# Conditioning scale and shift of the first norm: two-column TensorE products in place of VectorE dot products

## The chip, the cores and the metric

The kernel runs on one core of one Trainium2 chip. The metric is the device time of one execution in microseconds (us). Profile times are us from the start of the span. Engines are named as the profile names them: PE is TensorE, DVE VectorE, ACT ScalarE, POOL GpSimd, SP SyncE, whose queue issues most loads.

## What is computed

Two token streams go through one layer, 1024 prompt tokens and 32 sample tokens, each stream with a conditioning vector `c` of 1024 values. The change touches only the first lines of the layer:

```python
def rmsnorm(x, g):
    return x * lax.rsqrt(jnp.mean(x * x, axis=-1, keepdims=True) + EPS) * g

def layer(x, c, S0, conv_prev, p):
    mod = (c @ w_mod + b_mod)[:, None, :]              # c: 1024, w_mod: 1024 x 6144
    sh1, sc1, g1, sh2, sc2, g2 = jnp.split(mod, N_MOD, axis=-1)
    h = rmsnorm(x, norm1_g) * (1 + sc1) + sh1
    m, S_new, buf = token_mixer(h, ...)                # first: h @ w_in
    ...
```

`sh1` and `sc1` are 1024 values for each stream. Everything that follows (a gated linear attention, a short convolution, a gated merge, a SwiGLU mixer) needs `h`.

## The kernel before, in words

Channels lie on the 128 partitions: the 1024 channels are 8 tiles (`KT`), and the 1056 tokens of both streams lie along the free dimension, in blocks of 384, 384 and 288. Every product with a large weight is made of three float32r products (`hi*hi`, `hi*lo`, `lo*hi`): ACT rounds a weight to its high half (`whi`, `hl`), POOL or DVE subtracts to get the low half (`wlo`, `hl`); activations are split likewise into two tiles (`xm`, `h`).

The 48 columns of `mod` (6 groups of 8 tiles of 128 channels) come from `mod_tile`. It loads 128 rows of the transposed `w_mod` (`wm`, 512 KB) and lets DVE take a dot product of 1024 elements along the free dimension with `cb`, the conditioning vector written out on all partitions. For the prompt's vector that copy is made by two PE products (`pscb`), for the sample's by a load.

The first stage goes through a list written by hand, `ORDER`. `x` loads a tile of tokens and squares it, `w` loads and splits a weight tile of the keys, `c` makes a scale column of the prompt (`scale_col`), `m` scales and splits an x tile (`scaled`, tiles `xm`), `g` is one step of the contraction for the keys, taken before the norm's factor is known (`kmajor`, seven PSUM banks `psk`, 21 products of 384 columns), `s0` sums the squares (`psq`), and `s1` spreads the reciprocal root over the partitions (`psb`, `rstd`). Then the `psk` banks are multiplied by `rstd` into `st`.

A second list, `ORDER2`, makes the eight shift columns of the prompt (`s`, `shift_col`), two weight tiles of the queries (`w`), and `h` for tile 0 to 7 (`h`: POOL multiplies x by `rstd`, ACT adds the shift and rounds, DVE makes the low half). Behind it stand five PSUM banks of `kmajor` over `h` (15 products a step) and two further query tiles (`late`, tiles `ps`, 48 products a tile). The sample's scale and shift columns are made after that (`scale_col(k, 1)`, `shift_col(k, 1)`), followed by the gate projection (`psa`) and the value products (`psv`), among which the other 32 columns of `mod` are made for both streams (`some_mods`, 64 dot products).

A scheduler orders the instructions of each engine; only the loads are held in the order of the program (`pin`). PSUM is two pools of four banks, `psm` and `psx`. The `wm` buffers are five, and some small weights and the masks share them.

Of the kernel before, what the change touches and what calls it, by code (L numbers as in the profile page):

```python
# [7 lines left out]
F32 = mybir.dt.float32  # L8
# [3 lines left out]
ALU = mybir.AluOpType  # L12

P = 128
D = 1024
KT = D // P
# [28 lines left out]
DGL = 4  # L45
SSETS = 1
DTB = 1
ORDER2 = "p0 p1 p2 p3 p4 p5 p6 p7 s0 s1 w0 s2 s3 w1 s4 h0 h1 h2 s5 h3 s6 h4 s7 h5 h6 h7 c1".split()
W_LO = ('dve', 'pool')
W1_LO = ('pool', 'dve', 'pool', 'pool')  # L50
ORDER = "x0 w0 c0 m0 x1 c1 m1 x2 w1 x3 c2 m2 x4 w2 w3 g0 c4 c3 g1 x5 m3 m4 x6 x7 s0 s1 g2 g3 c5 m5 c7 c6 m6 g4 m7 g5 g6 g7".split()

Q0, K0, G0, CB0, CC0, CH0, GA0, GB0 = 0, 4, 8, 16, 24, 32, 40, 48

# [14 lines left out]
def hybrid_trunk(  # L69
    ctx: ExitStack,  # L70
    tc: tile.TileContext,
    xT,
    c_row,
    w_modT,
    b_mod,
    norm_g,
# [21 lines left out]
    nc = tc.nc  # L98
# [4 lines left out]
    psm = ctx.enter_context(tc.tile_pool(name="psm", bufs=4, space=bass.MemoryType.PSUM))  # L103
    psx = ctx.enter_context(tc.tile_pool(name="psx", bufs=4, space=bass.MemoryType.PSUM))
# [16 lines left out]
    ones = const.tile([P, P], F32, name="ones")  # L121
    masks = const.tile([P, 2 * len(LEVELS) + 1, P], U8, name="masks")
    epst = const.tile([P, 1], F32, name="epst")
    bmod = const.tile([P, 48], F32, name="bmod")
    ngs = const.tile([P, 3, KT], F32, name="ngs")
# [3 lines left out]
    mods = const.tile([P, 2, 48], F32, name="mods")  # L129
# [4 lines left out]
    def mm(ps, lhsT, rhs, start, stop):  # L134
        nc.tensor.matmul(ps, lhsT, rhs, start=start, stop=stop)  # L135
# [13 lines left out]
    def nm(s):  # L149
        uid[0] += 1  # L150
        return f"{s}_{uid[0]}"
# [3 lines left out]
    def load(dst, src):  # L155
        ins = nc.sync.dma_start(dst, src)
        if pin[0]:
            tc.keep_in_program_order(ins)
# [32 lines left out]
    with tc.tile_pool(name="p1", bufs=1) as p1:  # L191
        SL = "s"
        NSL = 9
        cb = p1.tile([P, 2, D], F32, name="cb")
        b1 = const.tile([P, KT], F32, name="b1")
        am1 = const.tile([P, 2, KT], F32, name="am1")
# [6 lines left out]
        nc.vector.tensor_scalar(b1, bmod[:, 8:16], 1.0, None, op0=ALU.add)  # L203

        def cond(s):
            if s:
                load(cb[:, s, :], c_row[:, s * D : (s + 1) * D].to_broadcast([P, D]))
                return
            crow = p1.tile([1, D], F32, tag="wm", name=nm("crow"), bufs=5)
            load(crow, c_row[:, s * D : (s + 1) * D])  # L210
            for i in range(2):
                ps = psm.tile([P, 512], F32, tag="m", name=nm("pscb"))
                mm(ps, ones[0:1, :], crow[:, i * 512 : (i + 1) * 512], True, True)
                nc.vector.tensor_copy(cb[:, s, i * 512 : (i + 1) * 512], ps)

        pin[0] = True
        cond(0)

        def mod_tile(j, s=None):
            wm = p1.tile([P, D], F32, tag="wm", name=nm("wm"), bufs=5)  # L220
            load(wm, w_modT[j])
            for st in (0, 1) if s is None else (s,):
                junk = p1.tile([P, D], F32, tag="junk", name=nm("junk"), bufs=1)
                nc.vector.tensor_tensor_reduce(  # L224
                    junk, wm, cb[:, st, :], 1.0, 0.0, ALU.mult, ALU.add, mods[:, st, j : j + 1]
                )

        def scale_col(k, s):
            mod_tile(8 + k, s)
            nc.vector.tensor_scalar(  # L230
                am1[:, s, k : k + 1], mods[:, s, 8 + k : 9 + k], b1[:, k : k + 1], ngs[:, 0, k : k + 1],
                op0=ALU.add, op1=ALU.mult,
            )

        def shift_col(k, s):
            mod_tile(k, s)
            nc.vector.tensor_tensor(mods[:, s, k : k + 1], mods[:, s, k : k + 1], bmod[:, k : k + 1], op=ALU.add)

        HW = BO[2]
        xs, sqs, xm, ws = [], [], [], []  # L240
# [31 lines left out]
        def banks(keys):  # L272
            return {(i, b): ((psm, psx)[b]).tile([P, 512], F32, tag="mx"[b], name=nm("psk")) for i, b in keys}
# [3 lines left out]
        rstds = []  # L277

        def sums():
            psq = psx.tile([P, 512], F32, tag="x", name="psq")  # L280
            for c in range(9):
                n = min(P, T - c * P)
                for i, sq in enumerate(sqs):
                    mm(psq[:n, c : c + 1], sq[:, c * P : c * P + n], ones[:, 0:1], i == 0, i == len(sqs) - 1)
            nc.scalar.activation(msc[:, 0:8], psq[:, 0:8], AF.Sqrt, bias=epst, scale=1.0 / D)
            nc.scalar.activation(msc[:DS, 8:9], psq[:DS, 8:9], AF.Sqrt, bias=epst[:DS], scale=1.0 / D)
            nc.vector.reciprocal(msc, msc)
# [10 lines left out]
                nc.scalar.copy(rstd[:, c0 * P : c0 * P + w], psb[:, :w])  # L298

        pss = banks(((0, 0), (0, 1), (1, 0), (1, 1), (2, 0), (2, 1), (3, 0)))  # L300
        for item in ORDER:
            kind, k = item[0], int(item[1])
            if kind == "x":
                load_x(k)
            elif kind == "c":
                scale_col(k, 0)
            elif kind == "m":
                scaled(k)
            elif kind == "w":
                hl = [p1.tile([P, KT, P], F32R, name=nm("hl")) for _ in range(2)] if k == 3 else None  # L310
                ws.append(load_w(w_in[K0 + k], hl=hl, lo_eng=W1_LO[k]))
            elif kind == "g":
                kmajor(pss, ws, xm[k], k)
            elif kind == "s":
                (sums, spread)[k]()
# [16 lines left out]
        for i in range(4):  # L332
            tag, bufs = ("sq", 4) if i < 3 else (SL, NSL)
            stk.append(p1.tile([P, T], F32, tag=tag, name=nm("st"), bufs=bufs))
        for (i, b), t in pss.items():
            nc.vector.tensor_tensor(stk[i][:, blk(b)], t[:, : wd(b)], rstd[:, blk(b)], op=ALU.mult)

        ws2 = [ws[3]]
        for item in ORDER2:
            kind, k = item[0], int(item[1])  # L340
            if kind == "s":
                shift_col(k, 0)
            elif kind == "w":
                ws2.append(load_w(w_in[Q0 + k], lo_eng=W_LO[k]))
            elif kind == "c":
                cond(1)
            elif kind == "p":
                nc.scalar.activation(xs[k][:, :S], xs[k][:, :S], AF.Copy, scale=am1[:, 0, k : k + 1])
            else:
                hi, lo = (r1.tile([P, T + 2], F32R, tag="r1", name=nm("h")) for _ in range(2))  # L350
                h.append((hi, lo))
                xp, shk = xs[k][:, :S], mods[:, 0, k : k + 1]
                nc.gpsimd.tensor_tensor(xp, xp, rstd[:, :S], op=ALU.mult)
                nc.scalar.activation(hi[:, :S], xp, AF.Identity, bias=shk)
                nc.vector.scalar_tensor_tensor(
                    lo[:, :S], xp, shk, f(hi[:, :S]), op0=ALU.add, op1=ALU.subtract
                )
# [46 lines left out]
            gemm(w, h, ev, blocks=(0, 1))  # L404

        for k in range(KT):
            scale_col(k, 1)
            shift_col(k, 1)
            modulate_sample(k)

        A = p1.tile([6 * RANK, T], F32R, tag="sq", name="A", bufs=4)
        for b in range(NB):
# [3 lines left out]
            ps = psm.tile([P, 512], F32, tag="m", name=nm("psa"))  # L416
# [70 lines left out]
        for hd in range(H):  # L487
# [10 lines left out]
            for tt in range(9):  # L498
                n = P if tt < 8 else DS
                sl = slice(tt * P, tt * P + n)  # L500
                ps = psm.tile([P, 512], F32, tag="m", name=nm("psv"))
# [557 lines left out]
    def cols(q):  # L1059
        return slice(2 * q * CW, 2 * (q + 1) * CW)  # L1060
# [105 lines left out]
    for j in range(KT):  # L1166
        w = load_w(w_conv_out[j])
        for c in range(NCH):
# [3 lines left out]
            ps = psc()  # L1172
# [645 lines left out]
```

## Time and profile before

| | |
|---|---|
| median of 3 runs | 1935.99 us (1935.78 to 1937.6) |
| profiled execution, its own time | 1936.16 us |
| span of that execution | 1934.4 us |
| mean granted clock of PE | 0.98 |
| PE busy | 1834.0 us, 95% of the span |
| DVE busy | 1383.1 us, 71% |
| ACT busy, POOL busy | 788.0 us, 41%; 797.6 us, 41% |

Time and span differ by 1.8 us, which lies outside the first and the last instruction. A busy share is an average over stages with different limits. The change acts in the first 280 us, so the views below are of that stretch; they are to be read for who waits for whom there and for the clock that PE had.

### The profile page before, as it was taken

To read this page: it belongs to the slowest core of one execution; us is meant where nothing else is said; L and a number is where in the kernel's file an instruction comes from. 1 tells how busy PE (TensorE), PEld (TensorE's weight loads), DVE (VectorE), ACT (ScalarE), POOL (GpSimd) and SP (SyncE) were. 2 spreads that over 40 slices of the span, in tenths; PEclk is the share of its full clock that TensorE was granted. 3 is DMA by queue.
4 is the path that set the end of the run, shared out by engine and by line. 5 is a ranking of instruction groups with operands and counts; after the bars stand their busy time and mean duration, and the time that the engine had idled before them with its cause. 6 is when DMAs were issued, how large, how long until landed. Compare 5 with 4: busy or idle time off the path is not lost. (4 is left out here: it accounts for less than half of the span.)

```text
span 1934.4 us, 35506 instructions
## 1 busy us (share of the span) xinstructions
PE 1834.0 (95%) x13517; PEld 1808.9 (94%) x13517; DVE 1383.1 (71%) x2543; ACT 788.0 (41%) x1641; POOL 797.6 (41%) x649
## 2 busy tenths in 40 slices
PE   6799899999999979999999999899999999999997
PEld 5689889899999979999999999899999999999997
DVE  7999967786875378543114478779988988678865
ACT  5434344444443145544212256444444444322243
POOL 6754447574762352212433243113223222255574
PEclk9799999999999989999999999999999999999998
DMA  7586643322322217424854455213443434586522
GB/s 275 182 292 229 212 165 123 93 83 77 100 77 77 76 61 233 152 106 167 318 184 146 134 161 161 80 56 128 154 153 128 153 143 143 203 313 235 212 95 90
DMA packets 166269, 298.45 MB, mean 154 GB/s; under 512 B 20593, under 2 KB 81905, under 8 KB 166098
## 3 DMA queue, kind: packets, MB, share of 16 engines
q1 hardware_dynamic: 117170, 211.90, 33.7%
q10 hardware_dynamic: 48928, 84.27, 11.7%
q8 instruction: 106, 1.74, 0.4%
q14 instruction: 65, 0.53, 0.1%
HBM read 211.78 MB, written 84.33 MB: 153 GB/s over the span
## 5 line engine op out<-in xcount | busy, mean ns | idle before, releaser
L135 PE MATMUL ps<-h,whi 128*128 128x384 f32 (+2 forms) x1440 | 350.3, 328 | 5.7 <-DVE vst L518 3.6
L143 POOL TENSOR_TENSOR wlo<-raw,whi 128x512 fp32r<-128x512 f32 (+2 forms) x160 | 220.7, 1398 | 312.7 <-ACT whi L139 214.1
L1327 PE MATMUL psX<-op,wg 128*128 128x264 f32 (+1 forms) x2112 | 273.1, 286 | 6.5 <-DVE bz L1358 4.2
L1327 PEld LDWEIGHTS psX<-op,wg 128*128 128x128 f32 x2112 | 264.1, 189 | 9.2 <-DVE bz L1358 6.1
L135 PEld LDWEIGHTS ps<-h,whi 128*128 128x128 f32 x1440 | 256.2, 193 | 6.7 <-issue 3.9
L940 POOL TENSOR_TENSOR wg<-raw,wg 128x512 fp32r<-128x512 f32 x66 | 96.3, 1459 | 366.9 <-ACT wg L939 301.6
L135 PE MATMUL ps<-h,wlo 128*128 128x384 f32 (+2 forms) x720 | 236.7, 329 | 0.0
L135 PE MATMUL ps<-u,whi 128*128 128x264 f32 (+2 forms) x1064 | 225.2, 305 | 2.3 <-ACT whi L139 1.7
L135 PEld LDWEIGHTS ps<-u,whi 128*128 128x128 f32 x1064 | 175.3, 188 | 3.3 <-ACT whi L139 2.0
L135 PE MATMUL ps<-u,wlo 128*128 128x264 f32 (+2 forms) x532 | 162.1, 305 | 0.0
L224 DVE CUSTOM_DVE_ANT_0 junk<-wm,cb 128x1024 f32<-128x1024 f32 x96 | 152.9, 1593 | 5.5 <-DMA wm<-in_w_modT 4.0
L1327 PE MATMUL psV<-op,wg 128*128 128x264 f32 (+1 forms) x1056 | 138.0, 286 | 1.0 <-ACT wg L939 1.0
L135 PEld LDWEIGHTS ps<-h,wlo 128*128 128x128 f32 x720 | 138.4, 192 | 0.4 <-issue 0.2
L1052 PE MATMUL psH<-u,wg 128*128 128x264 f32 x1056 | 133.9, 286 | 2.7 <-ACT wg L939 2.7
L139 ACT CAST whi<-raw 128x512 fp32r<-128x512 f32 (+2 forms) x164 | 87.5, 578 | 116.5 <-PE ps L135 56.1
L1327 PEld LDWEIGHTS psV<-op,wg 128*128 128x128 f32 x1056 | 133.3, 189 | 1.3 <-ACT wg L939 1.3
L1052 PEld LDWEIGHTS psH<-u,wg 128*128 128x128 f32 x1056 | 131.2, 190 | 3.3 <-ACT wg L939 3.3
L939 ACT CAST wg<-d 128x512 fp32r<-128x512 f32 x132 | 81.4, 621 | 109.7 <-PE psV L1327 36.8
L940 DVE TENSOR_TENSOR wg<-d,wg 128x512 fp32r<-128x512 f32 x121 | 93.8, 777 | 42.7 <-ACT wg L939 42.5
L1052 PE MATMUL psH<-h,wg 128*128 128x264 f32 x792 | 101.9, 287 | 6.2 <-ACT d L945 6.2
L1608 PE MATMUL psX<-u,wg 128*128 128x264 f32 x768 | 106.2, 284 | 0.0
L1052 PEld LDWEIGHTS psH<-h,wg 128*128 128x128 f32 x792 | 99.3, 191 | 6.5 <-ACT d L945 6.5
(321 smaller groups left out, 4008.4 us busy)
## 6 DMA issues: line engine op xcount, KB each, us to landing
wm<-in_w_modT SPq DMA_DIRECT2D x64, 512.0 KB, 4.6
raw<-in_w_in SPq DMA_DIRECT2D x124, 256.0 KB, 3.1
op_d<-st ACTq DMA_DIRECT2D x56, 528.0 KB, 5.7
u<-op_d SPq DMA_DIRECT2D x56, 528.0 KB, 6.2
raw<-in_w_ffn_in SPq DMA_DIRECT2D x88, 256.0 KB, 3.2
u<-og_d SPq DMA_DIRECT2D x16, 528.0 KB, 8.5
raw<-in_w_o SPq DMA_DIRECT2D x32, 256.0 KB, 3.2
raw<-in_w_ffn_out SPq DMA_DIRECT2D x32, 256.0 KB, 5.3
```

The costliest lines, as they stand in the source:

```text
L135: nc.tensor.matmul(ps, lhsT, rhs, start=start, stop=stop)
L139: nc.scalar.copy(hi, raw)
L143: nc.gpsimd.tensor_tensor(lo, raw, f(hi), op=ALU.subtract)
L224: nc.vector.tensor_tensor_reduce(junk, wm, cb[:, st, :], 1.0, 0.0, ALU.mult, ALU.add, mods[:, st, j : j + 1])
L939: nc.scalar.copy(hi, src)
L940: lo_eng.tensor_tensor(lo, src, f(hi), op=ALU.subtract)
L1052: nc.tensor.matmul(bank[i][q], wt[l][:, k, :], h_operand(i, k, q, r), start=i in (B11, B21, T3) and k == 0 and n == 0, stop=k == 3 and n == 2,
L1327: nc.tensor.matmul(ps, l[:, k, :], r[:, k, :], start=first and k == 0 and i == 0, stop=k == 3 and i == 2, skip_group_check=True,)
L1608: nc.tensor.matmul(ps, w[l][:, k, :], o[k][:, r, c], start=first and k == 0 and i == 0, stop=k == n - 1 and i == 2, skip_group_check=True,)
```

## The change

The 16 columns of shift and scale leave `mod_tile`. Their part of `w_mod` comes in a second layout, `w_modP`, contraction on the partitions, and `cc` holds both conditioning vectors as two columns for each contraction tile. For one column tile PE makes 8 products of a 128 x 128 weight with a 128 x 2 operand, in float32 without a split, into two columns of a PSUM bank (`psd` for the scale, `psd2` for the shift). One small DVE instruction then finishes both streams. The sample's columns therefore come with the prompt's, and the 16 separate loads for them are gone. `psd` takes the fourth bank of `psx`; the sums of squares move into it, and `s1` moves behind `m7`, since `psb` needs that bank. Both rows of `cb` are now loaded (`c0 c1`).

```diff
-ORDER2 = "p0 ... s7 h5 h6 h7 c1".split()
+ORDER2 = "p0 ... s7 h5 h6 h7 c0 c1".split()
-ORDER = "... x6 x7 s0 s1 g2 g3 c5 m5 c7 c6 m6 g4 m7 g5 g6 g7".split()
+ORDER = "... x6 x7 s0 g2 g3 c5 m5 c7 c6 m6 g4 m7 s1 g5 g6 g7".split()
...
+        def mod_cols(ps, j):
+            wm = p1.tile([P, KT, P], F32, tag="wm", name=nm("wm"), bufs=5)
+            load(wm, w_modP[j])
+            o = ps[:, 2 * (j % KT) : 2 * (j % KT) + 2]
+            for k in range(KT):
+                mm(o, wm[:, k, :], cc[:, k, :], k == 0, k == KT - 1)
+            return o
-        def scale_col(k, s):
-            mod_tile(8 + k, s)
+        def scale_col(k):
+            o = mod_cols(psd, 8 + k)
             nc.vector.tensor_scalar(
-                am1[:, s, k : k + 1], mods[:, s, 8 + k : 9 + k], b1[:, k : k + 1], ngs[:, 0, k : k + 1],
-                op0=ALU.add, op1=ALU.mult,
+                am1[:, :, k], o, b1[:, k : k + 1], ngs[:, 0, k : k + 1], op0=ALU.add, op1=ALU.mult
             )
-        def shift_col(k, s):
-            mod_tile(k, s)
-            nc.vector.tensor_tensor(mods[:, s, k : k + 1], mods[:, s, k : k + 1], bmod[:, k : k + 1], op=ALU.add)
+        def shift_col(k):
+            o = mod_cols(psd2, k)
+            nc.vector.tensor_scalar(mods[:, :, k], o, bmod[:, k : k + 1], None, op0=ALU.add)
...
-            psq = psx.tile([P, 512], F32, tag="x", name="psq")
+            psq = psd[:, 16:32]
...
         for k in range(KT):
-            scale_col(k, 1)
-            shift_col(k, 1)
             modulate_sample(k)
```

The scheduler's order changes with it. On PE, where `h` of the third tile is used: before, its products stand as follows (`psk_638` to `psk_642` are the five banks, `h_568` and `h_569` the high and low half of the tile, `hl_225`, `whi_523` and `whi_543` high halves of the weights).

```order
L135 MATMUL psk_642<-h_564,whi_543 128x384
L135 MATMUL psk_642<-h_563,wlo_544 128x384
L135 MATMUL psk_638<-h_568,hl_225 128x384
L135 MATMUL psk_639<-h_568,whi_523 128x384
L135 MATMUL psk_640<-h_568,whi_523 128x384
L135 MATMUL psk_641<-h_568,whi_543 128x384
L135 MATMUL psk_642<-h_568,whi_543 128x384
```

With the change the same place reads as follows (`psk_730` to `psk_734` are the banks, `h_641` and `h_642` the halves of the third tile, `wlo_611` the low half of the second query tile; `psd_547` is the bank `psd2`).

```order
L137 MATMUL psk_732<-h_636,wlo_579 128x384
L137 MATMUL psd_547<-cc,wm_599 128x2 x8
L137 MATMUL psk_730<-h_641,hl_238 128x384
L137 MATMUL psk_731<-h_641,whi_578 128x384
L137 MATMUL psk_732<-h_641,whi_578 128x384
L137 MATMUL psk_730<-h_642,hl_238 128x384
L137 MATMUL psk_730<-h_641,hl_239 128x384
L137 MATMUL psk_731<-h_642,whi_578 128x384
L137 MATMUL psk_731<-h_641,wlo_579 128x384
L137 MATMUL psk_732<-h_642,whi_578 128x384
L137 MATMUL psk_732<-h_641,wlo_579 128x384
L137 MATMUL psd_547<-cc,wm_620 128x2 x8
```

A shift column stands ahead of each tile's products, and for the first tiles the products of banks 733 and 734 (the second query tile) are put off until `wlo_611` is there. Ahead of the first product with the low half of the third tile (`h_569` before, `h_642` now) stood 39 of the second list's 216 products of 384 columns; now 29 stand there, with four of the shift columns, and the other 187 stand behind it with the other four. The scale columns from `c2` on, six of them, stand among the 168 products for the keys, behind the first 12 of them. The second of the three `psb` groups now has 21 key products and the third group behind it; before, all key products were ahead of it.

On POOL, at the start of the second list, before (`wlo_544` is the low half of the second query tile, `x_145` to `x_305` the eight x tiles):

```order
L253 TENSOR_TENSOR ssq_135<-ssq_135,sq_307 128x1056
L143 TENSOR_TENSOR wlo_544<-raw_545,whi_543 128x512
L143 TENSOR_TENSOR wlo_544<-raw_549,whi_543 128x512
L353 TENSOR_TENSOR x_145<-x_145,rstd 128x1024
L353 TENSOR_TENSOR x_167<-x_167,rstd 128x1024
```

and with the change (`x_325` and `x_330` are the last two of the tiles):

```order
L358 TENSOR_TENSOR x_325<-x_325,rstd 128x1024
L358 TENSOR_TENSOR x_330<-x_330,rstd 128x1024
L145 TENSOR_TENSOR wlo_611<-raw_612,whi_610 128x512
L145 TENSOR_TENSOR wlo_611<-raw_616,whi_610 128x512
L365 TENSOR_TENSOR xsm<-x_140,rstd 128x32
```

The low half moved from ahead of the eight multiplications to behind them.

On DVE, from the last key products to the low half of the first tile, before (`st` are the scaled key banks, `h_559` the low half of the first tile, `junk` rows are dot products):

```order
L336 TENSOR_TENSOR st_496<-psk_143,rstd 128x384
L237 TENSOR_TENSOR mods<-mods,bmod 128x1
L224 ISA junk_910,mods<-wm_908,cb 128x1024
L224 ISA mods 128x1
L363 TENSOR_TENSOR h_559<-mods,h_558 128x2
L355 SCALAR_TENSOR_TENSOR h_559<-x_145,mods,h_558 128x1024
```

and with the change (`wlo_579` is the low half of the first query tile, `h_632` that of the first tile of `h`):

```order
L340 TENSOR_TENSOR st_537<-psk_134,rstd 128x384
L147 TENSOR_TENSOR wlo_579<-raw_580,whi_578 128x512
L340 TENSOR_TENSOR st_537<-psk_135,rstd 128x384
L147 TENSOR_TENSOR wlo_579<-raw_584,whi_578 128x512
L340 TENSOR_TENSOR st_538<-psk_136,rstd 128x384
L340 TENSOR_TENSOR st_538<-psk_137,rstd 128x384
L340 TENSOR_TENSOR st_539<-psk_138,rstd 128x384
L240 TENSOR_SCALAR mods<-psd_547,bmod 128x2
L367 CAST h_631<-mods 128x2
L368 TENSOR_TENSOR h_632<-mods,h_631 128x2
L360 SCALAR_TENSOR_TENSOR h_632<-x_140,mods,h_631 128x1024
```

The dot products are gone from between; the two subtractions of the first query tile, which stood ahead of all `st` before, now stand among them.

## Rows read from the trace of the kernel before

**Rows 1.** Windows: busy us of each engine, then PEclk, DMA share, GB/s.

```profile
0.00:20.00 20.00, 6.00 (x10) 2.80 (x10) 10.27 (x12) 8.06 (x10) 8.35 (x9) 1.00 0.84 299
20.00:40.00 20.00, 16.45 (x74) 14.38 (x73) 17.14 (x17) 15.67 (x19) 17.06 (x7) 0.91 0.84 318
40.00:60.00 20.00, 19.85 (x115) 19.75 (x114) 19.82 (x35) 9.02 (x14) 4.91 (x3) 0.91 0.69 235
60.00:80.00 20.00, 9.71 (x39) 8.58 (x37) 20.00 (x22) 7.68 (x10) 20.00 (x8) 0.74 0.46 152
125.00:260.00 135.00, 122.45 (x933) 119.39 (x931) 130.03 (x160) 51.63 (x95) 64.52 (x28) 0.96 0.70 235
```

**Rows 2.** Timeline, marks on the way: start us, length us, instruction, idle before.

```profile
9.10 1.64 DVE L224 CUSTOM_DVE_ANT_0 junk<-wm,cb 128x1024 f32<-128x1024 f32 x1 [2.36 <-DMA wm<-in_w_modT]
...
60.54 1.05 PE L135 MATMUL psb<-ident,msc 128*128 128x128 f32 x8
...
67.34 0.69 PE L135 MATMUL psk<-h,hl 128*128 128x384 f32 x1 [4.66 <-ACT h L354]
...
122.08 5.76 PE L135 MATMUL psa<-h,wa 128*96 128x384 f32 x32
```

**Rows 3.** Timeline of PE, first and last of six products in a row.

```profile
39.78 0.34 PE L135 MATMUL psk<-xm,whi 128*128 128x384 f32 x1
...
40.65 0.34 PE L135 MATMUL psk<-xm,wlo 128*128 128x384 f32 x1
```

**Rows 4.** Timeline of PE: one near the start, then first and last of eight.

```profile
19.24 0.52 PE L135 MATMUL psk<-xm,wlo 128*128 128x384 f32 x1
...
74.06 0.53 PE L135 MATMUL psk<-h,wlo 128*128 128x384 f32 x1
...
76.30 0.53 PE L135 MATMUL psk<-h,hl 128*128 128x384 f32 x1
```

**Rows 5.** Timeline of PE: the nine float32 one-column products of the sums.

```profile
46.06 1.99 PE L135 MATMUL psq<-ones,ssq 128*128 128x1 f32 x18
```

**Rows 6.** Windows, as in Rows 1, around a change of the granted clock.

```profile
49.70:53.20 3.50, 3.50 (x13) 3.50 (x13) 3.50 (x7) 3.00 (x6) 0.00 (x0) 0.51 1.03 393
53.20:56.00 2.80, 2.80 (x18) 2.80 (x17) 2.77 (x8) 0.78 (x1) 0.00 (x0) 1.00 0.76 241
```

**Rows 7.** Timeline of POOL at the start of the second list.

```profile
59.69 3.06 POOL L143 TENSOR_TENSOR wlo<-raw,whi 128x512 fp32r<-128x512 f32 x2 [15.01 <-PE psk L135]
62.71 23.67 POOL L353 TENSOR_TENSOR x<-x,rstd 128x1024 f32<-128x1024 f32 x8
```

**Rows 8.** Timeline of DVE, 57 to 89.

```profile
57.89 1.29 DVE L145 TENSOR_TENSOR wlo<-raw,whi 128x512 fp32r<-128x512 f32 x2
...
63.83 1.48 DVE L336 TENSOR_TENSOR st<-psk,rstd 128x384 f32<-128x384 f32 x3
...
67.19 2.32 DVE L363 TENSOR_TENSOR h<-mods,h 128x2 fp32r<-128x2 f32 x1
69.43 3.44 DVE L355 SCALAR_TENSOR_TENSOR h<-x,mods,h 128x1024 fp32r<-128x1024 f32 x1
72.80 2.33 DVE L362 CAST h<-mods 128x2 fp32r<-128x2 f32 x1
...
78.45 3.35 DVE L355 SCALAR_TENSOR_TENSOR h<-x,mods,h 128x1024 fp32r<-128x1024 f32 x1
...
87.46 1.28 DVE L355 SCALAR_TENSOR_TENSOR h<-x,mods,h 128x1024 fp32r<-128x1024 f32 x1
```

**Rows 9.** Groups of instructions from 0 to 125: busy us, mean ns, idle before.

```profile
L224 DVE CUSTOM_DVE_ANT_0 junk<-wm,cb 128x1024 f32<-128x1024 f32 x34 | 54.5, 1602 | 4.0 <-DMA wm<-in_w_modT 4.0
```

**Rows 10.** Timeline of PE from 140 to 266: three that waited for DVE or ACT.

```profile
187.49 0.39 PE L135 MATMUL psv<-vhi,h 128*128 128x256 f32 x1 [1.88 <-ACT vst L516]
...
222.75 0.51 PE L135 MATMUL ps<-h,whi 128*128 128x290 f32 x2 [2.31 <-DVE vst L518]
...
265.45 0.39 PE L135 MATMUL psv<-vhi,h 128*128 128x256 f32 x1 [2.33 <-ACT vst L516]
```

More of the change, by code (lines that the diff above doesn't have):

```diff
@@ L47 @@
 DTB = 1
-ORDER2 = "p0 p1 p2 p3 p4 p5 p6 p7 s0 s1 w0 s2 s3 w1 s4 h0 h1 h2 s5 h3 s6 h4 s7 h5 h6 h7 c1".split()
+ORDER2 = "p0 p1 p2 p3 p4 p5 p6 p7 s0 s1 w0 s2 s3 w1 s4 h0 h1 h2 s5 h3 s6 h4 s7 h5 h6 h7 c0 c1".split()
 W_LO = ('dve', 'pool')
 W1_LO = ('pool', 'dve', 'pool', 'pool')
-ORDER = "x0 w0 c0 m0 x1 c1 m1 x2 w1 x3 c2 m2 x4 w2 w3 g0 c4 c3 g1 x5 m3 m4 x6 x7 s0 s1 g2 g3 c5 m5 c7 c6 m6 g4 m7 g5 g6 g7".split()
+ORDER = "x0 w0 c0 m0 x1 c1 m1 x2 w1 x3 c2 m2 x4 w2 w3 g0 c4 c3 g1 x5 m3 m4 x6 x7 s0 g2 g3 c5 m5 c7 c6 m6 g4 m7 s1 g5 g6 g7".split()
 Q0, K0, G0, CB0, CC0, CH0, GA0, GB0 = 0, 4, 8, 16, 24, 32, 40, 48
@@ L73, in hybrid_trunk @@
     c_row,
+    c_col,
+    w_modP,
     w_modT,
@@ L205, in cond, with mod_tile @@
         def cond(s):
[L206 to L214, printed above, removed]
+            load(cb[:, s, :], c_row[:, s * D : (s + 1) * D].to_broadcast([P, D]))
         pin[0] = True
-        cond(0)
-        def mod_tile(j, s=None):
+        cc = p1.tile([P, KT, 2], F32, name="cc")
+        load(cc, c_col)
+        def mod_tile(j):
             wm = p1.tile([P, D], F32, tag="wm", name=nm("wm"), bufs=5)
-            load(wm, w_modT[j])
-            for st in (0, 1) if s is None else (s,):
+            load(wm, w_modT[j - 16])
+            for st in (0, 1):
                 junk = p1.tile([P, D], F32, tag="junk", name=nm("junk"), bufs=1)
@@ L300, in hybrid_trunk @@
         pss = banks(((0, 0), (0, 1), (1, 0), (1, 1), (2, 0), (2, 1), (3, 0)))
+        psd = psx.tile([P, 512], F32, tag="x", name="psd")
         for item in ORDER:
@@ L305, in hybrid_trunk @@
             elif kind == "c":
-                scale_col(k, 0)
+                scale_col(k)
             elif kind == "m":
@@ L336, in hybrid_trunk @@
             nc.vector.tensor_tensor(stk[i][:, blk(b)], t[:, : wd(b)], rstd[:, blk(b)], op=ALU.mult)
+        psd2 = psx.tile([P, 512], F32, tag="x", name="psd2")
         ws2 = [ws[3]]
@@ L341, in hybrid_trunk @@
             if kind == "s":
-                shift_col(k, 0)
+                shift_col(k)
             elif kind == "w":
@@ L345, in hybrid_trunk @@
             elif kind == "c":
-                cond(1)
+                cond(k)
             elif kind == "p":
@@ L1773 @@
         "c_row": c(np.concatenate([g["c_prompt"][0], g["c_sample"][0]])[None]),
-        "w_modT": c(g["w_mod"][0].T).reshape(48, P, D),
+        "c_col": c(np.stack([cols(g["c_prompt"][0]), cols(g["c_sample"][0])], axis=2)),
+        "w_modP": pack(g["w_mod"][0][:, : 2 * D]),
+        "w_modT": c(g["w_mod"][0][:, 2 * D :].T).reshape(32, P, D),
         "b_mod": cols(g["b_mod"][0]),
```

## The prediction

> **What bounds the kernel now.** I read the windows first. PE is busy for 95% of the whole span, but the change acts where it is not: in 0–20 it is busy 6.0 us, in 60–80 9.7 us, while in 20–60 it lacks 3.7 us and in 125–260 12.5 us [rows 1]. DVE is full from 40 to 80 and nearly so to 260. The reader should see three stretches. In the first, up to the last spread of the sums at 60.54 + 1.05 = 61.6 [rows 2], PE starts late (the first dot product waits for its load until 9.10) and then has little idle time: PE is the bound. In the second, from the first product with `h` at 67.34 to `psa` at 122.08, PE waits for halves of `h`. In the third, PE runs ahead of work that DVE and ACT still owe it.
>
> Then the rate of one product. Six products of 384 columns start 0.87 us apart from first to last, 0.174 each [rows 3]; eight with the granted clock at half start 2.24 apart, 0.32 each, and one at 19.24 has the length of those [rows 4]. The one number nearest to a new column is the stretch of float32 one-column products: nine products, 18 passes, 1.99 us, so 0.111 a pass [rows 5].
>
> Last the DVE rows under POOL's work. POOL multiplies eight tiles in 23.67 us from 62.71, to 86.4 [rows 7]. In just that time DVE's small operations are long: a subtraction of two columns takes 2.32, a cast of two columns 2.33, the low half of a tile 3.44 and 3.35; at 87.46, with POOL past it, the low half takes 1.28 [rows 8]. So the third tile's low half, at 87.46 + 1.28 = 88.7, is what PE's dense stretch starts from.
>
> **The change part by part.** *A column on PE.* 8 products are 16 passes, 16 x 0.111 = 1.77 us [rows 5]; at half clock by the ratio of the products 0.32/0.174, 3.26. The two-column pass itself is in no row; below it could be as short as a product of two columns in proportion to 384 (nearly nothing), above it is the half-clock value. I take 1.77, since there too each pass brings a new 128 x 128 weight.
>
> *First stretch.* Columns `c0` and `c1` run at half clock, as the product at 19.24 does: 9.1 + 6.5 = 15.6; 12 key products at 0.32, 3.8; `c2` 1.8 (to 3.3): 21.2. Then 156 key products at 0.174 are 27.1, five columns 8.9, `psq` and `psb` with 18 passes each 2.0 + 2.0: 61.2. Waits for the operands, 3.7 in 20–60 before [rows 1], I put at 1.0 (0 to 3.7), since DVE has lost its dot products there. For the clock: 1.7 us after `psq` the granted level is 0.51, which is 1.2 of 2.4 GHz, for 3.5 us, though PE is dense, and full behind it [rows 6]. 3.5 us at half make 11 products in place of 20: 1.6 us lost. I count that twice, after `psq` and after `c5 c7`, which stand together: 3.2 (0 to 8 with one for every column). End: 65.4 (60 to 73).
>
> *POOL.* It starts 1.1 us behind the second `psb` group now (62.71 against 61.6). With the change that group ends 21 products and the last group, 4.0 us, before the end: 61.4 + 1.1 = 62.5, the same as before. The whole gain of moving `s1` pays for the columns of the first stretch; without it the multiplications would start four us later. The eight end at 86.2 and the two subtractions moved behind them (3.06) at 89.3, ahead of where PE needs `wlo_611`.
>
> *DVE to the third tile.* From 62.5: seven `st` at 0.49, 3.4 [rows 8]. Two weight subtractions stand among them; apart from POOL they take 1.29 together, under it they are not shown, so 1.3 to 2 x 2.9, and I take 4.6, two of the 2.32: 70.5. The columns' own ends (65.4 + 3.5) are hidden under this. A tile is then a cast 2.33, a subtraction 2.32 and a low half 3.4: 8.1 if all are long, 78.6 and 86.7; the third, by then under POOL's shorter work, I put at 3.0 (1.6 to 8.1): 89.7, against 88.7. The dot products between them are gone, but their place is taken by small operations that wait. **+1.0** (-7 with 5.7 a tile and 1.3 for the subtractions, so 81; +6 to 95).
>
> A rule weighed here: the Trainium skill, "GPSIMD Engine Reference", section "Key points", says that GpSimd shares its SBUF interfaces with VectorE and contends with instructions that have two SBUF inputs. The `st` rows, which have one input in PSUM, keep their 0.49 under POOL, and the two-input rows do not, so this trace agrees; by the rule the weight subtractions, two SBUF inputs each, would be long, by the row at 57.89 alone they would be 1.3 and the sum 3.3 us less.
>
> *Second stretch.* Behind the third tile's low half stood 177 products, 177 x 0.174 = 30.8, and the stretch took 122.08 - 88.74 = 33.3, so 2.5 of waits. Now 187 products stand there, 32.5, with four columns, 7.1, and waits that I put at 1.0 (0 to 2.5), since DVE's dots no longer stand between the low halves: 40.6. **+7.3.** The clock: four columns, each 1.77 us, in dense work, like `psq` with its 1.99. I count two drops, 2 x 1.6 = **+3.2** (0 to 6.4). So `psa` at 122.1 + 11.5 = 133.6.
>
> *Third stretch.* 34 dot products took 54.5 us, 1.60 each [rows 9]. Of DVE's work 32 go, 51 us, some of it before 40, where DVE had time. PE's 12.5 us of idle time in 125–260 shows waits for `vst` by DVE and ACT, 1.88, 2.31, 2.33 [rows 10]. The order of PE there is the same as before, and with DVE ahead they can go; ACT's are not plainly DVE's fault, and some are a chain from PE and back. **-6** (0 to -12).
>
> Loads: 16 of 512 KB go, which the dense first 60 us had at shares to 0.84; I count no gain, since PE's own work bounds that stretch.
>
> *Sum.* 1936.2 (the profiled execution's time) + 1.0 + 7.3 + 3.2 - 6 = 1941.7; the median lies 0.2 below it, so **1941.5**, +5.5. About 0.2%, 3.9 us, is what a measurement of this kernel can tell from no change: slower is above 1939.9, faster below 1932.1.
>
> **The rivals.**
> *VectorE's lead pays in full.* All 12 us of idle time behind `psa` go: 1941.5 - 6 = 1935.5, no change. For it: DVE is busy 130.0 of 135 us there. Against it: two of the three rows name ACT.
>
> *The low halves come early.* DVE passes POOL's window with 5.7 us a tile, third tile at 81, a gain of 8.7: 1932.8, on the edge; a little more makes it faster. For it: the dots are gone. Against it: the casts and subtractions of two columns, which are still there, are long by themselves.
>
> *The column is cheap* (the other side). Passes with an operand of two columns pipeline better than `psq`'s. Each us that a column is shorter counts six times up to POOL's start and four times behind it. At 0.4 us a column: 10 x 1.37 + 3.2 of clock less = 1924.6. It decides from 9.4/10, a column of 0.83 us or 52 ns a pass. Against it: `psq`, at 111 ns.
> The Trainium skill, "TensorE: Matmul & The Clock Gate", section "Wait — 56ns, not 53.3ns?", puts the floor from start to start of small matmuls at about 25 ns; by it a column would be an estimated 0.4 us. No row here is near it.
>
> *The clock holds.* No drop in the second stretch: 1941.5 - 3.2 = 1938.3, no change.
> The same page, section "Why this matters for your kernels", advises a loop contiguous in K for thin products, else the clock oscillates. The change's eight products are so written, and by the rule the clock would hold and the time be that 1938.3. `psq`'s nine stood contiguous too, and the clock fell behind them.
>
> *Every column drops the clock.* Six times in the first stretch in place of twice (+6.4 on POOL's start) and four in the second (+3.2): 1951.
>
> **How the numbers follow.** The forecast, from 1937 to 1946: 0.44, of which 0.32 slower. Lead in full 0.12 and clock held 0.06, both no change. Low halves early 0.16 (0.10 faster, 0.06 the same). Column cheap 0.08, faster. Every column drops the clock 0.14, slower. Together faster 0.18, same 0.36, slower 0.46. The range is 1928 to 1951: it leaves out the cheap column and the upper half of the last case, and holds the lower bound of the early low halves together with part of the lead. The forecast's own range is 1937 to 1946.
>
> **What would show it.** A column's eight products from first to next start: 1.77 at full clock. POOL's first multiplication at 62.5. The casts and subtractions of two columns at over 2 us until 86. The third tile's low half at about 90, and `psa` at 134. The granted clock at half behind `psq`, behind `c5 c7`, and behind two of the last four shift columns. PE's idle time in the 138 us from `psa` on about half of 12.5. Wrong would be a column under 0.83, a third tile's low half before 81, or a lead that makes up all: the first would put the end of the keys near 54.

## The result and the profile after

The changed kernel takes 1949.72 us (median of 4 runs, 1947.71 to 1951.79); the kernel before 1936.76 (median of 4). The ratio is 1.0067 (95% interval 1.005 to 1.0085): slower by 13.0 us, inside the range and on the side that was forecast, but by more than twice the forecast's 5.5. The profiled execution took 1950.26 us, with a span of 1948.1, 13.7 longer than before.

The windows of the kernel after, busy us of each engine, then PEclk, DMA share and GB/s; they answer to [rows 1]:

```profile
0.00:20.00 20.00, 10.59 (x43) 10.51 (x44) 6.23 (x8) 11.64 (x14) 9.58 (x10) 1.00 0.89 310
20.00:40.00 20.00, 20.00 (x109) 19.93 (x109) 9.55 (x9) 10.97 (x14) 13.90 (x8) 1.00 0.79 287
40.00:60.00 20.00, 19.25 (x125) 19.05 (x124) 2.16 (x6) 4.32 (x7) 0.00 (x0) 0.91 0.30 99
60.00:80.00 20.00, 17.60 (x97) 17.51 (x96) 14.29 (x15) 9.36 (x14) 12.38 (x5) 0.76 0.25 85
80.00:100.00 20.00, 16.70 (x72) 15.93 (x72) 15.45 (x13) 3.76 (x4) 17.73 (x17) 0.59 0.40 130
100.00:125.00 25.00, 25.00 (x144) 25.00 (x145) 12.86 (x30) 9.53 (x19) 4.53 (x14) 0.85 0.46 144
```

DVE, full before from 40 on, now has idle time throughout: it is busy for 2.2 us of 20 in 40 to 60, and for 14.3 and 15.5 in the two stretches behind. PE is busy for 17.6 us in 60 to 80, before for 9.7, and yet later: from 60 to 125 it waits for less than 6 us in all, and it is slow, with a granted clock of 0.76, 0.59 and 0.85.

PE's timeline of the kernel after, up to the end of the keys (start us, length us, instruction, idle before):

```profile
9.03 3.58 PE L137 MATMUL psd<-cc,wm 128*128 128x2 f32 x16 [9.03 <-DMA wm<-in_w_modP]
...
20.40 3.41 PE L137 MATMUL psd<-cc,wm 128*128 128x2 f32 x16
23.67 1.31 PE L137 MATMUL psk<-xm,whi 128*128 128x384 f32 x3
...
25.09 0.52 PE L137 MATMUL psk<-xm,whi 128*128 128x384 f32 x1
25.41 0.52 PE L137 MATMUL psk<-xm,wlo 128*128 128x384 f32 x1
...
29.33 1.84 PE L137 MATMUL psd<-cc,wm 128*128 128x2 f32 x16
...
50.24 1.95 PE L137 MATMUL psd<-cc,wm 128*128 128x2 f32 x16 [0.38 <-DVE am L234]
...
54.05 0.53 PE L137 MATMUL psk<-xm,wlo 128*128 128x384 f32 x1
54.37 0.53 PE L137 MATMUL psk<-xm,whi 128*128 128x384 f32 x1
...
59.58 1.96 PE L137 MATMUL psb<-ident,msc 128*128 128x128 f32 x8 [0.37 <-DVE am L234]
61.19 2.19 PE L137 MATMUL psk<-xm,whi 128*128 128x384 f32 x6
...
70.59 1.93 PE L137 MATMUL psd<-cc,wm 128*128 128x2 f32 x16
```

Products start 0.32 apart at 25.09, as at half clock in [rows 4], and again at 54.05 behind the two columns that stand together; the column at 20.40 takes 3.27 to the next start. Behind `c6` the `psb` group at 59.58 takes 1.61 to the next start, and the six products behind it are 0.34 apart. The keys end at 70.6, not at 65.4. (The granted clock in the windows says 1.00 for 0 to 40 all the same; here the distance of the starts is the safer reading.)

The same timeline from there to the gate projection `psa`:

```profile
74.92 3.58 PE L137 MATMUL psd<-cc,wm 128*128 128x2 f32 x16 [2.40 <-DVE mods L240]
78.35 0.67 PE L137 MATMUL psk<-h,hl 128*128 128x384 f32 x1
...
89.27 1.01 PE L137 MATMUL psk<-h,hl 128*128 128x384 f32 x2 [2.91 <-DVE h L360]
...
91.99 3.41 PE L137 MATMUL psd<-cc,wm 128*128 128x2 f32 x16
95.26 0.67 PE L137 MATMUL psk<-h,hl 128*128 128x384 f32 x1
...
98.29 3.41 PE L137 MATMUL psd<-cc,wm 128*128 128x2 f32 x16
101.55 0.67 PE L137 MATMUL psk<-h,hl 128*128 128x384 f32 x1
...
108.02 1.84 PE L137 MATMUL psd<-cc,wm 128*128 128x2 f32 x16
109.72 0.42 PE L137 MATMUL psk<-h,whi 128*128 128x384 f32 x1
...
141.41 5.77 PE L137 MATMUL psa<-h,wa 128*96 128x384 f32 x32
```

The first product with `h` stands at 78.35 against 67.34, `psa` at 141.41 against 122.08 [rows 2]: 19.3 later. A column takes 108.02 to 109.72, 1.70 us, at full clock, and 98.29 to 101.55, 3.26, at half. Of the 19.3 the rest of the program gives back 5.6: from `psa` to the end of the span are 1806.7 us, before 1812.3.

POOL and DVE in the same stretch (they answer to [rows 7, 8]):

```profile
67.62 20.50 POOL L358 TENSOR_TENSOR x<-x,rstd 128x1024 f32<-128x1024 f32 x8 [29.70 <-ACT rstd L301]
```

```profile
69.09 1.50 DVE L147 TENSOR_TENSOR wlo<-raw,whi 128x512 fp32r<-128x512 f32 x1
...
75.61 2.27 DVE L368 TENSOR_TENSOR h<-mods,h 128x2 fp32r<-128x2 f32 x1
77.80 3.48 DVE L360 SCALAR_TENSOR_TENSOR h<-x,mods,h 128x1024 fp32r<-128x1024 f32 x1
...
85.77 3.44 DVE L360 SCALAR_TENSOR_TENSOR h<-x,mods,h 128x1024 fp32r<-128x1024 f32 x1
...
91.53 1.35 DVE L360 SCALAR_TENSOR_TENSOR h<-x,mods,h 128x1024 fp32r<-128x1024 f32 x1
```

The pattern is that of before: a low half takes 3.5 under POOL's multiplications, 1.35 behind them. The third tile's low half is there at 92.9.

### The profile page after: what moved, and what is told of

Read it like the earlier page. It is cut to its first block, busy times and chain, and to the rows that moved or that the text cites. A ratio compares the mean times of both kernels' runs of the same rounds, so it can differ in the third digit from the quotient of the medians.

```text
span 1948.1 us, 35911 instructions
## 1 busy us (share of the span) xinstructions
PE 1869.1 (96%) x13769; PEld 1849.3 (95%) x13769; DVE 1326.6 (68%) x2461; ACT 789.0 (41%) x1641; POOL 772.9 (40%) x649
## 3 DMA queue, kind: packets, MB, share of 16 engines
q8 instruction: 108, 1.77, 0.4%
## 5 line engine op out<-in xcount | busy, mean ns | idle before, releaser
L145 POOL TENSOR_TENSOR wlo<-raw,whi 128x512 fp32r<-128x512 f32 (+2 forms) x160 | 214.3, 1359 | 310.0 <-ACT whi L141 239.8
L942 ACT CAST wg<-d 128x512 fp32r<-128x512 f32 x132 | 81.6, 623 | 110.8 <-PE psV L1330 33.7
L137 PEld LDWEIGHTS ps<-u,wlo 128*128 128x128 f32 x532 | 100.0, 188 | 0.8 <-POOL wlo L145 0.5
```

The costliest lines, as they stand in the source:

```text
L145: nc.gpsimd.tensor_tensor(lo, raw, f(hi), op=ALU.subtract)
L942: nc.scalar.copy(hi, src)
```

## The experiments

Two theories stood against each other. A: the two-column products leave PE's clock at half for the dense products behind them, and that is most of the loss. B: PE waits for the chain of DVE operations that POOL's multiplications slow, and the clock follows from the waits. Each run was timed beside the kernel before; ratios are to it. The scheduler may place other instructions anew with an edit; where it did so visibly, the text says so. Unless a profile row is named, times such as "`psa` at 130.5" are read from PE's timeline of that run. That timeline is of one execution; the executions of one kernel lie some 6 us apart (1938.32 to 1944.48 in the first run below), so a few us between a timeline and a median are no finding.

**A wide operand.** All 16 columns stay on PE, but each product reads the two conditioning columns 64 times over:

```diff
-            o = ps[:, 2 * (j % KT) : 2 * (j % KT) + 2]
+            q = P * (j % 3)
+            o = ps[:, q : q + 128].rearrange("p (r s) -> p r s", s=2)
...
-                mm(o, wm[:, k, :], cc[:, k, :], k == 0, k == KT - 1)
-            return o
+                mm(o, wm[:, k, :], cc[:, k : k + 1, :].to_broadcast([P, 64, 2]), k == 0, k == KT - 1)
+            return ps[:, q : q + 2]
...
-            psq = psd[:, 16:32]
+            psq = psd[:, 384:400]
```

> Each column product gets an operand of 128 columns (the two conditioning columns read 64 times over) in place of 2, with the same result in the first two columns; the bank is then used in three places of 128 columns, and nothing else is edited. Theory A (the two-column products leave PE's clock at half for the dense products behind them, 9 to 29, 52 to 56, 59 to 63 and 89 to 107 us of the profile after): a pass costs no more than the 0.10 of the 128-column float32 passes of psb, the granted clock is 1.00 from about 20 us on but where PE really waits, the gate projection starts at 128 to 133 in place of 141.4, and the time is 1936 to 1941. Theory B (PE waits for the low halves that DVE makes while POOL multiplies, and the clock follows from that): the half-clock stretch at 89 to 107 stays or shrinks little, the gate projection starts at 137 to 140, 1945 to 1949.

Measured: 1941.63, ratio 1.0019 (1.0009 to 1.0029), 8.1 below the change (9.3 by the ratios). PE's timeline of this run:

```profile
16.18 0.34 PE L137 MATMUL psk<-xm,wlo 128*128 128x384 f32 x1
16.35 0.34 PE L137 MATMUL psk<-xm,whi 128*128 128x384 f32 x1
...
19.06 1.95 PE L137 MATMUL psd<-cc,wm 128*128 128x128 f32 x16
20.77 0.42 PE L137 MATMUL psk<-xm,whi 128*128 128x384 f32 x1
...
69.86 3.46 PE L137 MATMUL psd<-cc,wm 128*128 128x128 f32 x16 [2.87 <-DVE mods L241]
...
130.46 1.74 PE L137 MATMUL psa<-h,wa 128*96 128x384 f32 x9
```

A column of 128 takes 19.06 to 20.77, 1.71, the same as one of two, and the products around it are 0.17 apart from 16 on, where the narrow kernel had 0.32 until 29. Half clock is left where PE had really waited, as at 69.86. The keys end at 64.95 (5.6 earlier), `psa` is at 130.46 (11.0 earlier, the middle of what A expected; the time is just above its band). That is what A says of the larger part of the loss. The width is not quite all that differs: the columns share three places of the bank, and the scheduler moved some key products, and the last three shift columns forward (behind 44, 65 and 86 of the second list's 216 products, not 56, 77 and 98). The same pair with other work on DVE, further down, gives a difference of the same size.

**One half of the change at a time.** Only the scale columns by PE, with the shift columns by `mod_tile` as before (the load `c0`, which their dot products need, goes to the head of the second list); and the other way round.

> Only the scale columns by PE (both streams), the shift columns by dot products on DVE as before. If the costs of the two halves add up: the end of the key products stays at 70.6, some 9 later than before, the second list runs as before (54.7 from its first product to the gate projection), and with 16 dot products less on DVE the later waits give back 2 to 4: 1941 to 1945. Theory A says that most of the 9 is clock (three stretches at half) and column time; theory B says that the later start of POOL's multiplications passes the 9 on in full: both the same here, and the run tells the halves apart. If the scale columns cost nothing (hidden by the idle first 20 us): 1934 to 1938.

Measured: 1941.76, ratio 1.0027 (1.0017 to 1.0036), `psa` at 131.0. The time is in the first band, but not by the way that the band was worked out: the keys end at 68.2, not 70.6, and the second list takes 62.7 up to `psa`, not 54.7. PE waits there for DVE, which has the dot products, the `st` and the low halves to do beside POOL's multiplications:

```profile
79.11 0.66 PE L137 MATMUL psk<-h,whi 128*128 128x384 f32 x1 [10.53 <-DVE st L340]
```

> Only the shift columns by PE (both streams), the scale columns by dot products on DVE as before, the sums and their spread where they stood before. The key products end near 61, POOL's multiplications start near 62.7. Theory A: from the second shift column on the clock stays at half until about 100, the gate projection starts at 129 to 133, and with the later waits cut by 2 to 4 the time is 1940 to 1945. Theory B: the columns fill the time in which PE waited for low halves before (10.4 us), so only those behind the third tile cost, 4 to 5 times 1.7: the gate projection at 125 to 129, 1934 to 1940.

Measured: 1935.91, ratio 0.9996 (0.9984 to 1.0007), no change; `psa` at 131.4, as A said, while the time is B's: from `psa` to the end 1802.1 us, 10.2 less than before. The delays of `psa`, 8.9 and 9.3, sum to 18.2, against 19.3 with both halves. That is no proof that the halves add up, since most of the first is the wait for DVE, which the change does not have. In the medians they do not: 5.2 and -0.8 by the ratios, against 13.0. Why the shift half alone gets back so much behind `psa` was not tried, and stays open.

**The shift half with a wide operand.**

> The kernel with only the shift columns by PE, each product with an operand of 128 columns. Theory A (thin products pull the clock down): the half-clock stretch from 74 to 99 us of the narrow kernel shrinks to the time in which PE really waits for low halves, the gate projection starts at 123 to 128 in place of 131.4, the time is 1927 to 1933. Theory B (waits for DVE's low halves set that clock): PE still waits at 73 and 81, the clock stays at half till 95 or later, 129 to 131, and 1933 to 1936.

Measured: 1934.41, ratio 0.9984 (0.9974 to 0.9993). `psa` is at 122.1, 9.3 earlier than with the narrow operand, and the clock is 1.00 in 80 to 100, where the narrow run had 0.66. The narrow run's window, then the wide one's:

```profile
80.00:100.00 20.00, 18.95 (x88) 18.95 (x89) 9.37 (x13) 3.45 (x3) 8.36 (x11) 0.66 0.26 91
80.00:100.00 20.00, 19.93 (x137) 19.61 (x136) 12.48 (x23) 5.79 (x7) 6.87 (x13) 1.00 0.34 114
```

The median fell by only 1.5 (2.3 by the ratios), into B's band. A is right on the stretch and wrong on the time: what comes first is not kept to the end. The profiled execution, the fastest of its ten, is 4.7 below the narrow one: 9.3 less up to `psa`, 4.6 more behind it (1806.7 us). Where the rest went was not tried.

**The multiplications moved from POOL to DVE**, first as they are:

```diff
-                nc.gpsimd.tensor_tensor(xp, xp, rstd[:, :S], op=ALU.mult)
+                (nc.vector if k in (0, 1, 2, 3, 4, 5, 6, 7) else nc.gpsimd).tensor_tensor(xp, xp, rstd[:, :S], op=ALU.mult)
```

> The changed kernel with the eight multiplications of x by the norm's factor moved from POOL to DVE, so that POOL is idle beside DVE's low halves; the scheduler moves the late query tiles in among the tiles with it. Theory B: casts and subtractions of two columns fall from 2.2 to 0.2 us and low halves from 3.4 to 1.3, the first two low halves are there some 5 to 9 us earlier, the gate projection starts at 132 to 136 and the time is 1940 to 1945. Theory A: PE is at half clock with its columns through that stretch and bound by itself, the gate projection starts at 138 to 141, 1946 to 1949.

Measured: 1952.38, ratio 1.0076 (1.0061 to 1.0092). Neither theory's time. DVE of this run, and then PE:

```profile
68.34 7.95 DVE L358 TENSOR_TENSOR x<-x,rstd 128x1024 f32<-128x1024 f32 x5
...
85.36 0.21 DVE L240 TENSOR_SCALAR mods<-psd,bmod 128x2 f32<-128x2 f32 x1
85.60 0.17 DVE L367 CAST h<-mods 128x2 fp32r<-128x2 f32 x1
85.80 0.16 DVE L368 TENSOR_TENSOR h<-mods,h 128x2 fp32r<-128x2 f32 x1
86.78 1.28 DVE L360 SCALAR_TENSOR_TENSOR h<-x,mods,h 128x1024 fp32r<-128x1024 f32 x1 [0.82 <-ACT h L359]
```

```profile
85.62 3.58 PE L137 MATMUL psd<-cc,wm 128*128 128x2 f32 x16 [12.37 <-DVE mods L240]
```

The lengths are what B said: 0.17, 0.16 and 1.28 with POOL out of the way. But the scheduler put all eight multiplications ahead of the finish of the first column, and the second column waited 12.4 us for it. So the multiplication and the low half were then held in turn (`keep_in_program_order` on both), in three kernels.

> As the one before, and the eight multiplications of x by the norm's factor are moved from POOL to DVE and held in turn with the low halves, so that POOL does not work beside them; the scheduler puts seven of the columns ahead of the first product with h. If POOL's work beside DVE is the rest of the cost (the part of theory B that a held clock leaves): casts of two columns 0.2, low halves 1.3, no wait of PE for a low half longer than 1 us, the columns run in one piece at 62 to 76, the gate projection starts at 114 to 119, the time is 1922 to 1929. If DVE's added 10 us are what comes out instead: as the run before, within 2 us.

Measured: 1925.84, ratio 0.9941 (0.9926 to 0.9955): the lowest median of this study, 0.6% under the kernel before. No wait for a low half is left, but `psa` is at 121.3, later than expected, since the seven columns in one piece, each with 0.32 of wait for the finish of the one before, kept the first products with `h` back to 81.6.

> The kernel before, all columns by dot products on DVE, with the multiplications moved from POOL to DVE and held in turn with the low halves: what that move is worth without the columns on PE. DVE is full there from 40 to 258, so the 10 us of multiplications come on top of it: if DVE is the bound of that stretch, the third tile's low half is no earlier than 86 and the time 1936 to 1944; if POOL's work beside it was the bound, the third tile's low half is at 78 to 82 and the time 1928 to 1934.

Measured: 1929.98, ratio 0.9955 (0.9941 to 0.9969): this edit alone is worth most of that, with all dot products on DVE. The third tile's low half:

```profile
81.85 1.27 DVE L355 SCALAR_TENSOR_TENSOR h<-x,mods,h 128x1024 fp32r<-128x1024 f32 x1
```

It ends at 83.1, 5.6 earlier than before, and `psa` is at 114.8, 7.3 earlier. By the medians the gain at the end is 7.4 us (in the profiled execution, the slowest of its five, 3.0). So POOL's work beside DVE held the low halves up in the kernel before, more than the dot products did: with those of the shift columns gone and POOL as before, the third tile's low half was at 85.8, 3.0 earlier. The edit also holds the multiplications and low halves in turn; that order with the multiplications left on POOL was not run. The intervals of this run and the one above overlap a little.

> All 16 columns by PE with an operand of 128 columns, and the multiplications on DVE in turn with the low halves. By theory A and the POOL part of B together: keys end at 65 as in the run with the wide operand, seven columns stand ahead of the first product with h, the gate projection starts at 118 to 123 in place of 130.5, and the time is 1926 to 1933. If the wait of the second shift column for DVE's finish of the first (2.9 us with the wide operand) grows, since DVE has more to do there: 1934 to 1940.

Measured: 1930.66, ratio 0.9966 (0.9953 to 0.9979), `psa` at 124.4, just behind its first band, and the time within it: the wait of the second column for the finish of the first is 0.7 here.

**The same, narrow again.**

> All 16 columns by PE with the operand of two columns as in the change, the multiplications on DVE in turn with the low halves: the run with the wide operand and those multiplications (1930.66, gate projection at 124.4), narrow again. Theory A says the clock falls behind the columns whether DVE makes PE wait or not: six columns stand in one piece behind the keys, the granted clock is half behind them and in three stretches ahead of 60, the gate projection at 130 to 136, the time 1936 to 1942. If only PE's waits set the clock (theory B): as with the wide operand, within 2 us.

Measured: 1941.96, ratio 1.0028 (1.0018 to 1.0038), `psa` at 135.3: 11.3 above the wide one (12.0 by the ratios). From its timeline of PE:

```profile
76.61 3.57 PE L137 MATMUL psd<-cc,wm 128*128 128x2 f32 x16 [0.31 <-DVE mods L240]
80.50 3.57 PE L137 MATMUL psd<-cc,wm 128*128 128x2 f32 x16 [0.31 <-DVE mods L240]
```

and from that of the wide one:

```profile
77.24 2.05 PE L137 MATMUL psd<-cc,wm 128*128 128x128 f32 x16 [0.32 <-DVE mods L241]
79.60 2.05 PE L137 MATMUL psd<-cc,wm 128*128 128x128 f32 x16 [0.32 <-DVE mods L241]
```

The waits are the same, 0.3 each, and the clock is not. The windows behind, of the narrow run and of the wide one:

```profile
80.00:100.00 20.00, 19.06 (x93) 18.80 (x94) 11.11 (x23) 6.87 (x12) 5.13 (x6) 0.62 0.52 159
80.00:100.00 20.00, 17.77 (x111) 17.13 (x111) 17.46 (x32) 9.12 (x17) 7.22 (x9) 1.00 0.51 166
```

PE was busy for longer in the narrow run, and had the lower clock. That speaks against B's half of the claim, that the clock follows from the waits alone. (The scheduler put six columns together here and seven there. That a wait can come ahead of half clock too is shown at 69.86 in the first run.)

**The order of DVE written out**: finish of a column, multiplication of that tile, low half of the tile before.

> Only the shift columns by PE with an operand of 128 columns, the multiplications on DVE, and the order of DVE written out: finish of a shift column, multiplication of that tile, low half of the tile before it. The run with seven columns in one piece started its first product with h only at 81.8; here four columns stand ahead of the dense products. If PE alone is then the bound from the end of the keys (61 to 64) on, with 216 products of 0.174, eight columns of 1.7 and 3 us of waits: the gate projection at 116 to 119, the time 1920 to 1925. If DVE still makes PE wait (finish, multiplication and low half are 2.9 us a tile): 1925 to 1928, no better than the run with the seven columns.

Measured: 1928.58, ratio 0.9957 (0.9942 to 0.9971). `psa` at 118.8 as expected, the time just above the second reading's band although DVE makes PE wait only 0.3 to 0.6 at a time: behind `psa` it takes 1807.2. Its interval overlaps that of the run with seven columns in one piece, so the two are not told apart.

> The same with all 16 columns by PE, operand of 128 columns. The keys end at 65, 3 later than with the scale columns on DVE, the gate projection comes at 118 to 122 and the time is 1923 to 1928, 2 to 4 above the run with the shift columns alone. If the wide operand and the removed work of POOL leave no cost in the scale columns: equal within 1 us.

Measured: 1934.54, ratio 0.9988 (0.9978 to 0.9998), above both its bands: the second column waited 2.9 us for the finish of the first again, and `psa` came at 124.7.

Three pairs of runs with the wide operand differ in the scale half alone: 1941.63 against 1934.41, 1930.66 against 1925.84, and this one against 1928.58. Each time PE's scale columns cost 4.8 to 6.8 us by the ratios, although no operand is thin there. So the scale half of the change is a loss by itself here.

**Both first shift columns ahead of their finish**, in the change as it is:

```diff
-            if kind == "s":
+            if kind == "s" and k == 0:
+                continue
+            elif kind == "s" and k == 1:
+                oo = [mod_cols(psd2, j) for j in (0, 1)]
+                for j in (0, 1):
+                    nc.vector.tensor_scalar(mods[:, :, j], oo[j], bmod[:, j : j + 1], None, op0=ALU.add)
+            elif kind == "s":
                 shift_col(k)
```

> The change as it is, but the first two shift columns are both made before DVE finishes either, so that the second no longer waits 2.4 us for the finish of the first in the same bank. Theory A, with PE and its clock as the bound of that stretch: the columns end at 74 to 75 in place of 78.4, the gate projection comes 2 to 4 earlier, 1945 to 1948. Theory B, with the chain of DVE operations under POOL's work as the bound up to the second tile's low half (89.3): that low half is no earlier, the idle time of PE only moves, 1948 to 1950.

Measured: 1944.38, ratio 1.004 (1.0027 to 1.0054), 5.3 less than the change, below both bands, with `psa` at 136.1. B was wrong on the second tile's low half, which ends at 86.5 in place of 89.2; but the third tile's is hardly earlier, 92.5 against 92.9. The gain lies behind it:

```profile
88.92 3.58 PE L137 MATMUL psd<-cc,wm 128*128 128x2 f32 x16 [4.62 <-DVE mods L240]
...
97.24 1.84 PE L137 MATMUL psd<-cc,wm 128*128 128x2 f32 x16
98.94 0.60 PE L137 MATMUL psk<-h,wlo 128*128 128x384 f32 x2
```

A third column now stands with the first two, ahead of the products. One column fewer lies among the products at half clock (88.92, where the change has 91.99 and 98.29), and products are 0.17 apart again from about 96.5 in place of 107.3, although the longest wait of PE is now 4.62. So the place of the columns seems to count more by the clock that they leave than by the wait that they take; no run changes the one without the other.

## Why the prediction was right, and where it was too small

The forecast's own band, 1937 to 1946, was missed by 3.7 us. The range held the measured time because it reached up to the case of the rivals in which every column drops the clock (1951, 0.14).

**First stretch, the step that failed by 5.1.** POOL was to start at 62.5; it started at 67.62, with the chain as described (rstd from the second `psb` group). The size of the clock's term was wrong, 3.2 us for two stretches at half, and so were its places:

- At the start some 30 products ran at half, not 12, and `c2` too: about 4 us more than forecast (18 products at 0.146 each, 1.5 for `c2`).
- Behind `psq`, from which the estimate was taken [rows 6], the clock did not fall at all.
- Behind `c5 c7` it was at half from about 52.9 to 56.3, 3.4 us, as forecast; that is 1.5 us lost.
- Behind `c6` it fell for the `psb` group and six products, 59.6 to 63.2, about 1.8 us lost, which the forecast did not have.

Together that is about 7.3 in place of 3.2. Most of what is left of the 5.1 is `c0` and `c1`, which took 7.4 and not 6.5. The rival in which every column drops the clock came nearest in its time, but not in what happened: the clock was full behind the columns at 29.33, 34.79, 108.02, 113.47 and 118.95. That its number was nearly hit is luck.

**DVE to the third tile, right within 2 us.** 27.2 us from POOL's start were forecast, 25.3 measured (67.62 to 92.88). The long casts and subtractions were there (2.09, 2.27), the two weight subtractions took 1.50 and 2.36 where 4.6 was taken for both. By the Trainium skill ("GPSIMD Engine Reference", "Key points") operations with two SBUF inputs contend with GpSimd; for the subtractions this trace agrees, with 0.65 each apart from POOL [rows 8]. Two inputs are not the whole of it here: a cast has one, and took 2.09.

**A step overlooked.** The two first columns were called hidden under DVE's work. In fact the second waits for the finish of the first, as both lie in one bank (2.40 at 74.92), and then runs at half clock, so that the first product with `h` came at 78.35. In the last run this wait is gone; the second tile's low half came 2.7 earlier there, the third tile's 0.4.

**Second stretch, too small by 4.7.** From the third tile's low half to `psa` 43.8 us were forecast (40.6 and a clock term of 3.2), 48.5 measured. The column's price was right (1.70 against 1.77; 3.26 at half, as forecast). The path was not: PE did not wait for that low half. When it was there, at 92.88, PE was at its fourth shift column, at half clock, until 95.26, so the dense stretch began 2.4 later. And PE stayed at half from 89 to 107 in one piece, where two drops of 3.5 us were forecast: behind 95.26 some 25 products and the column at 98.29 lost about 5.2 us by it, not 3.2.

**Third stretch, right in its number.** 6 us given back were forecast, 5.6 measured. The forecast looked for them in PE's idle time of the 138 us behind `psa`. There PE was idle for 9.6 us, before for 12.6, so 3.0 of them; the rest comes from later, which the forecast had not reckoned with.

So the direction held, and the price of a column. The mis-sized term is the clock: most of the 5.1 and 4.7 too little in the two stretches, less the 1.9 by which DVE's chain came out shorter. The run with the wide operand takes 8.1 us out of the median; in its profiled execution the keys end 5.6 earlier and the stretch from there to `psa` is 5.3 shorter. The cheap column is out (1.70, not under 0.83). The lead of VectorE did not pay in full. The low halves did not come early. That the clock holds because the eight products stand contiguous in K, as the Trainium skill ("TensorE: Matmul & The Clock Gate", "Why this matters for your kernels") advises for thin products, is not what this trace shows: they stand so in `c5` and `c7`, the products ahead of them ran 0.17 apart, and those behind them 0.32.

## What to carry to other kernels

When small work moves to TensorE, price it by the clock of the dense work behind it too: here the thin products' own 1.7 us each were foreseen, and the half clock that they left, some 8 us more over all 16 columns, was priced too low. Where such a product takes as long with a wide operand as with a thin one (1.71 against 1.70 here), try the wide one: it took 8.1 and 11.3 us off with all 16 columns, but only 1.5 with the shift columns alone. And before work is moved off a full engine, look at what makes its operations long: here moving eight multiplications away from POOL and holding them in turn with the low halves, beside the same dot products, was worth more (0.9955) than the change meant to relieve VectorE (1.0067).

## What was not expected of the hardware

A float32 product of a 128 x 128 weight took 0.106 to 0.107 us a pass with an operand of 2 as of 128 columns. PE's clock stayed at half from its start at 9 to 29 us with two-column products among the dense ones, by the distance of the starts (0.32), although PE was never idle for more than 0.4 us in that time; with the wide operand it was full from 16 (0.17). Two-column DVE operations on SBUF took up to 2.3 us beside POOL's multiplications and 0.16 without; the finish of a column, which reads PSUM, kept its 0.2.
